# Earlier first logits and a new spread of gate steps and splits in the stick-breaking stage of a two-layer decoder trunk

## The chip, the cores and the metric

The kernel runs on one core of one Trainium2 chip. The metric is the device time of one execution in microseconds (us). Of each kernel one execution is also profiled; its trace has its own time and span, and all durations in this text come from such a trace.

The engines are TensorE (PE in the profile; its weight loads are PEld), VectorE (DVE), ScalarE (ACT), GpSimd (POOL) and SyncE (SP), which here only starts DMAs. PE writes to PSUM, eight banks of 128 x 512 floats; ACT and DVE read from there.

## The reference

Two layers over 512 tokens of width 2048, all in float32, batch 1. Layer 0 is a sparse attention chosen by an indexer; layer 1 is a stick-breaking attention with 16 query heads and 4 shared key/value heads of width 128. Each layer adds its mixer to the scaled stream, normalises it and adds a gated embedding. The change touches layer 1's mixer only:

```python
def mixer_b(x, w_in, w_o, k, v):
    q, gate = jnp.split(x @ w_in, [WIDTH_B], axis=-1)
    ...
        z = jnp.einsum('bqngd,bsnd->bngqs', qg, k).astype(jnp.float32) * (HEAD_DIM ** -0.5)
        strict = key_pos[None, :] < t[:, None]
        log_om = jnp.where(strict, -jax.nn.softplus(z), 0.0)
        suffix = lax.cumsum(log_om, axis=log_om.ndim - 1, reverse=True) - log_om
        a = jnp.where(strict, jnp.exp(jax.nn.log_sigmoid(z) + suffix), 0.0)
        o = jnp.einsum('bngqs,bsnd->bqngd', a.astype(v.dtype), v)
    ...
    return (o * jax.nn.silu(gate)) @ w_o
```

So the stage needs q and gate (two products of 2048 by 2048 weights), then for each of 4 key heads, with 4 query heads each, logits, a softplus, a running sum over the keys from the right, an exponential, and the product with the values.

## The kernel before

**Numbers.** Every float32 operand of PE is split into a high part (a rounded copy, made by ACT) and a low part (the rest, made by DVE: `split`, L140). A product is three matmuls, high x high, high x low and low x high (`mm3`, L145 to L147). So each new operand costs one ACT and one DVE instruction before PE can use it. Weights come from DRAM in pairs of 128 x 512 blocks into three buffers `raw`, in the order of the list `units`, by loads on SP's queue; each load waits until its buffer has been read. Their parts `wh` and `wl` have three buffers each, so a weight can be split at most three ahead of the one that PE uses.

**The stages around the change.** The queries (`F[0]` to `F[3]`, one per group of four heads) are made by a Strassen product in five chunks (`gemm_s`; the first chunk makes the values). A chunk has 112 steps of three matmuls of 128 x 256. Strassen overwrites half of the columns of eight blocks of the stream (`XH`, `XL`) by sums; these halves are read back from DRAM (`x2`) and split again (`restore`) in the next stage. During a chunk, small pieces of work wait in the list `bg`, and `pumped_at` takes one from it at the listed steps: the adds that end the chunk before, and in the last chunk the splits of the values (`split_values`) and of the first group's keys (`split_keys`). The last chunk ends with `combine_last`: one copy on ACT, seven adds on DVE.

**The stick-breaking stage** has four groups. In each, PE makes the gate of the group (`gemm_w` or `gate_first`: 16 weights, four steps each, 64 gate steps of three matmuls) and in between the attention of that group's four heads in ten units (`Sticks.units`), a unit being one block of 128 queries against one block of 128 keys. What a unit needs is spread over turns (`Sticks.turn`, L1369):

- `logits`: three matmuls into a PSUM bank (two banks alternate; unit 0 of a group has a third); in diagonal units a mask is added by DVE,
- `soft`: three instructions on ACT (absolute value, exponential, logarithm), `plus`: one on DVE; together the softplus,
- `high`, `low`: its two parts on DVE, with the running total of the block row put in; ACT copies a row `t` of the logits,
- `weights`: two matmuls add the running sum onto the logits; ACT takes the exponential, DVE updates the total; only then is the bank free for the logits two units on,
- `halves`: the two parts of the exponential (ACT, DVE), `values`: three matmuls with the values, `leave`: a copy of the output to `F` by ACT.

Turn s issues the logits and softplus of unit s, the values of unit s-2 and the weights of unit s-1, with `gate(n)` putting n gate steps in between (three numbers for each turn in `TURNS`). `feed()` splits gate weights ahead (up to ten gate steps beyond the current one unless told otherwise), `others(n)` takes n pieces from `bg`.

**What sets the order.** PE's order is the order of the code. On ACT and DVE a scheduler orders what is free to move; `paced` keeps pieces in program order, and `strictly` puts each instruction behind the last strict one of its engine. All of the stick-breaking stage is strict, so one late instruction on ACT or DVE holds all behind it. Instructions of ACT and DVE are all issued in a helper and carry its lines in the profile: L116 if strict, L118 if not; they are told apart by their tiles.

Group 0 starts like this (L1427 on): the query splits 3 and 1 are held back behind the combining adds, nine gate steps run, then come the logits of units 0 and 1 with one gate step between them.

```python
    bg.extend(lambda i=i: after_combining(split_scaled, 0, i) for i in (3, 1))
    ...
    for n in range(9):
        gate(1)
        if bg:
            one()
        feed()
    strictly(sticks.logits, 0)
    gate(1)
    strictly(sticks.logits, 1)
```

At the boundary of two groups, PE goes on with the logits of units 0 and 1 of the next group and ten gate steps, while ACT and DVE close the old group (`close`: SiLU and product), change the activation table, and start the new softplus chains.

Of the kernel before, what the change touches and what calls it, by code (L numbers as in the profile page):

```python
# [10 lines left out]
F32 = mybir.dt.float32  # L11
F32R = mybir.dt.float32r
I32 = mybir.dt.int32
AF = mybir.ActivationFunctionType
ALU = mybir.AluOpType
# [62 lines left out]
def trunk_kernel(  # L78
# [61 lines left out]
    def split(hi, lo, src, eng=dve):  # L140
        act.activation(hi, src, AF.Copy)
        eng.tensor_tensor(lo, src, hi.bitcast(F32), ALU.subtract)
# [217 lines left out]
    def one():  # L360
        paced(bg.popleft())

    def pumped_at(gen, when):
        for i, _ in enumerate(gen):
            if bg and i in when:
                one()
            yield
# [203 lines left out]
    for g in range(4):  # L571
        add_job(w_in_b, g * 512, strassen=True)
    x2 = dram.tile([D, T], F32, name="x2")
    for k in (4, 5, 6, 7, None, 0, None, 1, 2, 3):
        if k is None:
            first = 4 * (units[-1][1] == 0)
            units.append((x2.rearrange("(k p) t -> p k t", p=128)[:, first : first + 4, H:T],))
        else:
            units.append((w_in_b, 2 * k, 2 * k + 1, D, 512))
# [599 lines left out]
        split(XH[k][:, H:T], XL[k][:, H:T], raw[:, k % 4])  # L1179

    def gate_items():
        for k, n in ((0, 8), (4, 2)):
            yield from plain_items([(512, n)])
            raw = next_raw()
            bg.extend(lambda raw=raw, k=k: restore(raw, k) for k in range(k, k + 4))
            if k:
                bg.append(lambda: split_keys(1))
        yield from plain_items([(512, 6), *[(512, NK)] * 3])

    C3.extend(c3_tiles(pc_.enter_context(tc.tile_pool(name="pc1", bufs=1))))  # L1190
    V, K = ([tuple(spots[n : n + 2]) for n in where] for where in ((0, 2, 4, 6), (8, 14) * 2))
    Q, A = ([tuple(spots[n : n + 2]) for n in where] for where in ((10, 12, 16, 18), (20, 22)))

    def split_keys(g):
        split(*K[g], Kf[:, g])

    def split_values(t):
        split(*(v.rearrange("p (g d) -> p g d", g=4) for v in V[t]), Vf[:, :, t * 128 : (t + 1) * 128])

    with tc.tile_pool(name="sp", bufs=1) as sp:  # L1200
        Kf, Vf = shared
        banks = [bank(b, "k") for b in range(4)]
        gemm = gemm_w(kitems, plain, banks, order=PAIRS)
        items = first_chunk(gemm, TF, T1, C3, lambda: strassen_stream([512] * 5, sp))
        for g in range(4):
            act.activation(Kf[:, g], banks[g], AF.Copy)

        def turn_values(t):
            s = slice(t * 128, (t + 1) * 128)
            ps = bank(2, "vt")  # L1210
            for g in range(4):
                pe.transpose(ps[:, g * 128 : (g + 1) * 128], Vf[:, g, s], ident)
            act.activation(Vf[:, :, s], ps.rearrange("p (g d) -> p g d", g=4), AF.Copy)

        for n, dst in enumerate((Vf, *F)):
            M = product_banks(4 - n)
            gemm = pumped_at(gemm_s(items, C3, M), (13, 20, 27, 34, 41, 53, 65, 77, 89, 101))
            if n == 1:
                steps(gemm, 40)
                for t in range(4):  # L1220
                    steps(gemm, 16)
                    turn_values(t)
            run(gemm)
            drain()
            if n == 4:
                items = Ahead(gate_items(), 2).prime()
                combined = combine_last(sp, M, lambda i: quarter(dst, i))
            else:
                bg.extend(combine(sp, M, lambda i: quarter(dst, i)))
            if n == 3:  # L1230

                bg.extend(lambda t=t: split_values(t) for t in range(4))
                bg.append(lambda: split_keys(0))

    pv_.close()
    px = pc_.enter_context(ss(name="px", bufs=1))

    def split_scaled(g, i):
        qh, ql = (q.rearrange("p (h q) -> p h q", h=4) for q in Q[i])
        src = F[g][:, :, i * 128 : (i + 1) * 128]  # L1240
        act.activation(qh, src, AF.Copy, scale=HSCALE)
        dve.scalar_tensor_tensor(ql, src, HSCALE, qh.bitcast(F32), ALU.mult, ALU.subtract)

    def gate_first(banks):

# [21 lines left out]
    class Sticks:  # L1267
# [101 lines left out]
        def turn(self, s, gaps):  # L1369

            late = self.diagonal(s)
            new = 1 < s < 10
            if new:
                strictly(self.logits, s)
                if late:
                    strictly(self.low, s - 1)
                strictly(self.soft, s)
                if not late:
                    strictly(self.plus, s)
                    feed(1)  # L1380
            gate(gaps[0])
            if s > 1:
                strictly(self.values, s - 2)
            gate(gaps[1])
            if s < 11:
                strictly(self.weights, s - 1)
                if new and late:
                    strictly(self.plus, s)
                strictly(self.halves, s - 1)
                if new:  # L1390
                    strictly(self.high, s)
                    if not self.diagonal(s + 1):
                        strictly(self.low, s)
            else:
                strictly(act.preload_act_table_set, "silu_and_others")
            if s > 1:
                strictly(self.leave, s - 2)

            if self.g < 3:
                bg.extend(lambda i=i: split_scaled(self.g + 1, i) for i in {8 if self.g == 0 else 6: (1,), 9: (3,), 10: (0,)}.get(s, ()))  # L1400
            feed()
            others(1 if self.g else 2)
            gate(gaps[2])

    def after_combining(fn, *args):
        with tc.issue_after(combined):
            fn(*args)

    gated = [0]

    def gate(n):
        steps(gemm, n)
        gated[0] += n

    def feed(most=9, ahead=10):

        while most and items.count < min(64, -(-(gated[0] + ahead) // 4)):
            strictly(items.push)
            most -= 1

    def others(n):
        for _ in range(min(n, len(bg))):
            strictly(bg.popleft())

    LOG_EXP = "natural_log_exp_and_others"
    tc.keep_in_program_order(act.preload_act_table_set(LOG_EXP))
    bg.extend(lambda i=i: after_combining(split_scaled, 0, i) for i in (3, 1))  # L1427
    banks = mm_banks("g")
    items = Fed(items)
    gemm = gate_first(banks)  # L1430
    sticks = Sticks(0)
    for n in range(9):
        gate(1)
        if bg:
            one()
        feed()
    strictly(sticks.logits, 0)
    gate(1)
    strictly(sticks.logits, 1)
    for u in range(2):  # L1440
        for fn in (sticks.soft, sticks.plus, sticks.high, sticks.low):
            strictly(fn, u)
        feed(1)
    bg.extend(lambda i=i: split_scaled(0, i) for i in (2, 0))
    for n in (3, 2, 2):
        gate(n)
        feed()
        others(1)

    TURNS = (  # L1450
        ((0, 0, 2), (1, 1, 3), (1, 1, 2), (1, 1, 2), (2, 1, 2), (1, 1, 2), (1, 1, 3), (2, 1, 2), (1, 1, 2), (1, 1, 2), (1, 1, 3)),
        ((0, 0, 3), *[(1, 1, 3)] * 3, (2, 1, 3), *[(1, 1, 3)] * 2, (2, 1, 3), (1, 1, 3), (1, 1, 2), (1, 1, 4)),
    )
    for g in range(4):
        for s in range(1, 12):
            if g and s == 2:
                bg.append(lambda g=g: split_scaled(g, 2))
            if 0 < g < 3 and s == 3:
                bg.append(lambda g=g: split_keys(g + 1))
            sticks.turn(s, TURNS[g > 0][s - 1])  # L1460
        gate(64 * (g + 1) - gated[0])
        others(len(bg))
        if g < 3:
            then = Sticks(g + 1)
            for u in range(2):
                strictly(then.logits, u)

        def close(h):
            sg = work()
            act.activation(sg, banks[h], AF.Silu)  # L1470
            dve.tensor_tensor(F[g][:, h], F[g][:, h], sg, ALU.mult)

        for h in range(4):
            strictly(close, h)
        if g < 3:
            sticks = then
            feed(1)
            strictly(act.preload_act_table_set, LOG_EXP)
            for u in range(2):
                for fn in (sticks.soft, sticks.plus, sticks.high, sticks.low):  # L1480
                    strictly(fn, u)
                feed(1)
            banks = mm_banks("g")
            gemm = gemm_w(items, plain, banks)
            for _ in range(5):
                gate(2)
                feed()
    pk_.close()
    pc_.close()

# [55 lines left out]
```

## Time and profile before

| what | us |
|---|---|
| median of 3 runs | 1875.55 (1875.39 to 1876.4) |
| profiled execution | 1875.82 |
| its span, first to last instruction | 1874.1 |
| PE busy | 1857.8 (99% of the span) |
| DVE busy | 1232.3 (66%) |
| ACT busy | 939.8 (50%) |

The mean granted clock of PE was 0.998. In the timeline of this trace the last Strassen matmul starts just before 1233.88, the first logits of group 0 at 1240.03, those of groups 1 to 3 at 1305.66, 1369.28 and 1432.88, and the output projection at 1497.78.

A row of the timeline gives start, duration, engine, line, operation, what is written and read, the shape, and in brackets how long the engine sat idle before it and which instruction ended that. `c` stands for all tiles cut from one big buffer: keys, values, queries and the halves of the exponential. `z` are logits, `wk` work tiles, `sh` and `sl` the parts of the softplus, `g` the gate's banks, `o` the output's. A row of the table of stretches gives the stretch, its length, the busy time of PE, PEld, DVE, ACT and POOL with the number of instructions, the granted clock, the busy share of the DMA engines, and GB/s. The table of waits gives total, times and longest. Matmuls overlap: one is shown with about 0.39 us while the next starts 0.23 after it.

### The profile page before, as it was taken

To read this page: it belongs to the slowest core of one execution; us is meant where nothing else is said; L and a number is where in the kernel's file an instruction comes from. 1 tells how busy PE (TensorE), PEld (TensorE's weight loads), DVE (VectorE), ACT (ScalarE), POOL (GpSimd) and SP (SyncE) were. 2 spreads that over 40 slices of the span, in tenths; PEclk is the share of its full clock that TensorE was granted. 3 is DMA by queue.
4 is the path that set the end of the run, shared out by engine and by line. 5 is a ranking of instruction groups with operands and counts; after the bars stand their busy time and mean duration, and the time that the engine had idled before them with its cause. 6 is when DMAs were issued, how large, how long until landed. Compare 5 with 4: busy or idle time off the path is not lost.

```text
span 1874.1 us, 24812 instructions
## 1 busy us (share of the span) xinstructions
PE 1857.8 (99%) x9181; PEld 1576.2 (84%) x9181; DVE 1232.3 (66%) x2395; ACT 939.8 (50%) x1696; POOL 4.7 (0%) x20
## 2 busy tenths in 40 slices
PE   9999999999999999999999999999999999999998
PEld 8898888888888888888888999987777888888887
DVE  5668678566556454675367788877877745567534
ACT  3546333355554432474245444468888743347422
POOL 0000000000000000000000000000000000000000
PEclk9999999999999999999999999999999999999999
DMA  6441333322222532333343333322122253243333
GB/s 197 127 121 60 102 91 101 92 66 68 68 68 66 162 110 79 124 102 108 117 133 116 104 100 111 103 79 79 56 68 71 71 185 101 73 129 94 120 101 113
DMA packets 111178, 189.21 MB, mean 101 GB/s; under 512 B 8528, under 2 KB 29008, under 8 KB 111056
## 3 DMA queue, kind: packets, MB, share of 16 engines
q1 hardware_dynamic: 111056, 187.62, 32.9%
q8 instruction: 72, 1.18, 0.3%
q14 instruction: 50, 0.41, 0.1%
HBM read 179.21 MB, written 8.39 MB: 100 GB/s over the span
## 4 chain that ended last, share of the span: by engine, by line
PE 93%; ACT 3%; DVE 2%; issue 1%; DMA 0%; SPq 0%; DVEq 0%; ACTq 0%
PE g L145 11%; PE g L147 11%; PE g L146 11%; PE o L145 7%; PE o L147 7%; PE o L146 7%; PE m L145 4%; PE m L147 4%; PE m L146 4%; PE q L145 3%; PE q L147 3%; PE q L146 3%; ACT wk L116 2%; PE k L147 2%; PE k L146 2%; PE k L145 2%
## 5 line engine op out<-in xcount | busy, mean ns | idle before, releaser
L118 ACT ACTIVATE wh<-raw 128x512 fp32r<-128x512 f32 (+2 forms) x624 | 359.5, 577 | 688.4 <-PE g L146 220.4
L118 DVE TENSOR_TENSOR wl<-raw,wh 128x512 fp32r<-128x512 f32 (+2 forms) x624 | 388.2, 623 | 439.6 <-ACT wh L118 424.9
L145 PE MATMUL g<-xh,wh 128*128 128x512 f32 x1024 | 404.3, 395 | 3.6 <-ACT wh L116 3.6
L147 PE MATMUL g<-xh,wl 128*128 128x512 f32 x1024 | 400.3, 391 | 0.0
L146 PE MATMUL g<-xl,wh 128*128 128x512 f32 x1024 | 399.9, 390 | 0.0
L147 PEld LDWEIGHTS g<-xh,wl 128*128 128x128 f32 x1024 | 192.5, 188 | 42.4 <-DVE wl L116 1.3
L145 PEld LDWEIGHTS g<-xh,wh 128*128 128x128 f32 x1024 | 192.8, 188 | 41.7 <-ACT wh L116 4.8
L146 PEld LDWEIGHTS g<-xl,wh 128*128 128x128 f32 x1024 | 192.8, 188 | 37.0
L146 PE MATMUL o<-xl,wh 128*128 128x512 f32 x512 | 199.2, 389 | 0.0
L145 PE MATMUL o<-xh,wh 128*128 128x512 f32 x512 | 199.2, 389 | 0.0
L147 PE MATMUL o<-xh,wl 128*128 128x512 f32 x512 | 199.2, 389 | 0.0
L147 PEld LDWEIGHTS o<-xh,wl 128*128 128x128 f32 x512 | 96.1, 188 | 20.1
L146 PEld LDWEIGHTS o<-xl,wh 128*128 128x128 f32 x512 | 96.1, 188 | 20.0
L145 PEld LDWEIGHTS o<-xh,wh 128*128 128x128 f32 x512 | 96.1, 188 | 19.9
L145 PE MATMUL q<-xh,wh 128*128 128x512 f32 x256 | 99.6, 389 | 0.0
L146 PE MATMUL q<-xl,wh 128*128 128x512 f32 x256 | 99.6, 389 | 0.0
L147 PE MATMUL q<-xh,wl 128*128 128x512 f32 x256 | 99.6, 389 | 0.0
L118 ACT ACTIVATE sh<-st 128x512 fp32r<-128x512 f32 x80 | 49.7, 624 | 44.2 <-DVE st L118 44.1
L116 ACT ACTIVATE wk<-z 128x512 f32<-128x512 f32 x80 | 47.6, 595 | 38.6 <-DVE z L116 16.2
L118 DVE TENSOR_TENSOR sl<-st,sh 128x512 fp32r<-128x512 f32 x80 | 55.1, 690 | 13.9 <-ACT sh L118 13.9
L118 DVE TENSOR_TENSOR xl<-f,xh 128x512 fp32r<-128x512 f32 x80 | 54.3, 685 | 12.6 <-ACT f L118 12.3
L147 PEld LDWEIGHTS q<-xh,wl 128*128 128x128 f32 x256 | 48.1, 188 | 10.0
(297 smaller groups left out, 3394.2 us busy)
## 6 DMA issues: line engine op xcount, KB each, us to landing
raw<-w_in_a SPq DMA_DIRECT2D x95, 512.0 KB, 3.7
raw<-w_in_b SPq DMA_DIRECT2D x64, 512.0 KB, 3.8
raw<-w_ple_gate SPq DMA_DIRECT2D x52, 512.0 KB, 3.7
raw<-w_o_a SPq DMA_DIRECT2D x24, 512.0 KB, 3.7
raw<-w_o_b SPq DMA_DIRECT2D x24, 512.0 KB, 3.7
raw<-w_kv_b SPq DMA_DIRECT2D x16, 512.0 KB, 3.8
raw<-w_ple_gate SPq DMA_DIRECT2D x24, 256.0 KB, 2.9
f<-xT SPq DMA_DIRECT2D x4, 1024.0 KB, 6.4
```

What stands on the lines that cost most here:

```text
L116: ins = method(*args, **kw)
L118: ins = method(*args, **kw)
L145: pe.matmul(out, a[0], b[0], start=start, stop=False)
L146: pe.matmul(out, a[0], b[1], start=False, stop=False)
L147: pe.matmul(out, a[1], b[0], start=False, stop=stop)
```

## The change

Seven edits, all around the stick-breaking stage.

1. The logits of unit 0 stand first in group 0, before any gate step; then come six gate steps, the logits of unit 1, five gate steps, and the turns.
2. The query splits 3, 1 and 2 of group 0 become pieces of the last Strassen chunk, pumped at steps 104, 107 and 110, behind the values and keys. Query part 3 moves to buffers that the chunk reads last in its fourth of eight rounds; part 0 takes the old buffers of part 3 and is split in turn 1.
3. All groups use one list `TURNS` of mostly five gate steps a turn. Group 0 had its own of mostly four.
4. `first_soft` puts a weight split (`feed(1, ahead)`) between the softplus of units 0 and 1 and their high and low parts, in all groups. At the boundaries the ten gate steps follow without feeds of their own.
5. In turns of diagonal units (5 and 8) only one weight is fed, and nothing is taken from `bg`.
6. The read-back of the first four half blocks from `x2` comes after three pairs of gate weights instead of four, the second after two more pairs instead of one.
7. `after_combining` goes.

```diff
-    for k in (4, 5, 6, 7, None, 0, None, 1, 2, 3):
+    for k in (4, 5, 6, None, 7, 0, None, 1, 2, 3):
...
-        for k, n in ((0, 8), (4, 2)):
+        for k, n in ((0, 6), (4, 4)):
...
-    Q, A = ([tuple(spots[n : n + 2]) for n in where] for where in ((10, 12, 16, 18), (20, 22)))
+    Q, A = ([tuple(spots[n : n + 2]) for n in where] for where in ((18, 12, 16, 10), (20, 22)))
...
-            gemm = pumped_at(gemm_s(items, C3, M), (13, 20, 27, 34, 41, 53, 65, 77, 89, 101))
+            gemm = pumped_at(gemm_s(items, C3, M), (13, 20, 27, 34, 41, 53, 65, 77, 89, 101, 104, 107, 110))
...
                 bg.append(lambda: split_keys(0))
+                bg.extend(lambda i=i: split_scaled(0, i) for i in (3, 1, 2))
...
-            feed()
-            others(1 if self.g else 2)
+            if new and late:
+                feed(1)
+            else:
+                feed()
+                others(1 if self.g else 2)
             gate(gaps[2])
...
+    def first_soft(u, ahead=18):
+        strictly(sticks.soft, u)
+        strictly(sticks.plus, u)
+        feed(1, ahead)
+        strictly(sticks.high, u)
+        strictly(sticks.low, u)
+
...
-    bg.extend(lambda i=i: after_combining(split_scaled, 0, i) for i in (3, 1))
...
-    for n in range(9):
-        gate(1)
-        if bg:
-            one()
-        feed()
     strictly(sticks.logits, 0)
-    gate(1)
-    strictly(sticks.logits, 1)
-    for u in range(2):
-        for fn in (sticks.soft, sticks.plus, sticks.high, sticks.low):
-            strictly(fn, u)
-        feed(1)
-    bg.extend(lambda i=i: split_scaled(0, i) for i in (2, 0))
-    for n in (3, 2, 2):
-        gate(n)
-        feed()
-        others(1)
-
-    TURNS = (
-        ((0, 0, 2), (1, 1, 3), (1, 1, 2), (1, 1, 2), (2, 1, 2), (1, 1, 2), (1, 1, 3), (2, 1, 2), (1, 1, 2), (1, 1, 2), (1, 1, 3)),
-        ((0, 0, 3), *[(1, 1, 3)] * 3, (2, 1, 3), *[(1, 1, 3)] * 2, (2, 1, 3), (1, 1, 3), (1, 1, 2), (1, 1, 4)),
-    )
+    for u, n in enumerate((6, 5)):
+        for _ in range(n):
+            gate(1)
+            if not u:
+                feed()
+        if not u:
+            strictly(sticks.logits, 1)
+            first_soft(0)
+            first_soft(1, 14)
+    bg.append(lambda: split_scaled(0, 0))
+
+    TURNS = ((0, 0, 3), *[(1, 1, 3)] * 3, (2, 1, 3), *[(1, 1, 3)] * 2, (2, 1, 3), (1, 1, 3), (1, 1, 2), (1, 1, 3))
...
             for u in range(2):
-                for fn in (sticks.soft, sticks.plus, sticks.high, sticks.low):
-                    strictly(fn, u)
-                feed(1)
+                first_soft(u)
             banks = mm_banks("g")
             gemm = gemm_w(items, plain, banks)
-            for _ in range(5):
-                gate(2)
-                feed()
+            gate(10)
```

More of the change, by code (lines that the diff above doesn't have):

```diff
@@ L1198, in split_values, with split_scaled @@
         split(*(v.rearrange("p (g d) -> p g d", g=4) for v in V[t]), Vf[:, :, t * 128 : (t + 1) * 128])
+    def split_scaled(g, i):
+        qh, ql = (q.rearrange("p (h q) -> p h q", h=4) for q in Q[i])
+        src = F[g][:, :, i * 128 : (i + 1) * 128]
+        act.activation(qh, src, AF.Copy, scale=HSCALE)
+        dve.scalar_tensor_tensor(ql, src, HSCALE, qh.bitcast(F32), ALU.mult, ALU.subtract)
     with tc.tile_pool(name="sp", bufs=1) as sp:
@@ L1233, in trunk_kernel @@
                 bg.append(lambda: split_keys(0))
+                bg.extend(lambda i=i: split_scaled(0, i) for i in (3, 1, 2))
     pv_.close()
     px = pc_.enter_context(ss(name="px", bufs=1))
[L1238 to L1242, printed above, removed]
     def gate_first(banks):
@@ L1400, in turn @@
                 bg.extend(lambda i=i: split_scaled(self.g + 1, i) for i in {8 if self.g == 0 else 6: (1,), 9: (3,), 10: (0,)}.get(s, ()))
-            feed()
-            others(1 if self.g else 2)
+            if new and late:
[3 more added lines that the diff above has]
+                others(1 if self.g else 2)
             gate(gaps[2])
-    def after_combining(fn, *args):
-        with tc.issue_after(combined):
-            fn(*args)
     gated = [0]
@@ L1459, in trunk_kernel @@
                 bg.append(lambda g=g: split_keys(g + 1))
-            sticks.turn(s, TURNS[g > 0][s - 1])
+            sticks.turn(s, TURNS[s - 1])
         gate(64 * (g + 1) - gated[0])
```

## The prediction

> **What bounds the kernel now.** I read the page's head first, then a table of stretches over the stick-breaking stage, then the list of waits of PE, and last the timelines of PE, DVE and ACT around the places that these named.
>
> ```profile
> span 1874.1 us, 24812 instructions
> ...
> PE 1857.8 (99%) x9181; PEld 1576.2 (84%) x9181; DVE 1232.3 (66%) x2395; ACT 939.8 (50%) x1696; POOL 4.7 (0%) x20
> ```
>
> TensorE is the bound: a change that leaves the matmuls as they are can only win what PE loses between them. A busy matmul hides part of that, so I count starts. These two rows stand 23 matmuls apart (one turn of five gate steps: 15 gate, 3 logits, 2 weights, 3 values), in a turn without a wait:
>
> ```profile
> 1323.01 0.39 PE L145 MATMUL z<-c 128*128 128x512 f32 x1
> ...
> 1328.22 0.39 PE L145 MATMUL z<-c 128*128 128x512 f32 x1
> ```
>
> 5.21 / 23 = 0.2265 us for each. A group of four heads has 64 x 3 gate matmuls and 10 x 8 of the sticks, 272, so it needs at least 61.7. The four groups, from the last Strassen matmul to the first matmul of the output projection:
>
> ```profile
> core 0: us, PE busy (x) PEld busy (x) DVE busy (x) ACT busy (x) POOL busy (x), PEclk, DMA share, GB/s
> 1233.88:1305.66 71.78, 66.16 (x275) 51.48 (x273) 55.32 (x95) 52.57 (x94) 1.23 (x6) 0.98 0.25 74
> 1305.66:1369.28 63.62, 62.61 (x274) 50.69 (x272) 50.00 (x82) 51.62 (x88) 0.00 (x0) 1.00 0.22 67
> 1369.28:1432.88 63.60, 62.59 (x274) 50.70 (x272) 50.01 (x82) 51.63 (x88) 0.00 (x0) 1.00 0.22 67
> 1432.88:1497.78 64.90, 62.93 (x274) 50.65 (x272) 50.14 (x81) 51.81 (x88) 0.00 (x0) 1.00 0.21 65
> ```
>
> Less 61.7 each, they lose 10.1, 1.9, 1.9 and 3.2: **17.1 us in all**, the most that this change can win here. The reader sees also that ACT and DVE need 50 to 55 us a group, not much less than PE, so their order decides. The waits behind the loss:
>
> ```profile
> PE g L145 <- ACT wh L116: 3.6, 3, 1.8
> PE z L145 <- DVE t L116: 3.2, 3, 1.8
> PE o L1359 <- ACT c L116: 1.7, 1, 1.7
> ```
>
> The first row is three group boundaries, the other two are group 0. The third has a sequel, a stretch at a lower granted clock:
>
> ```profile
> 1249.78:1257.50 7.72, 5.57 (x16) 3.79 (x15) 5.95 (x10) 6.00 (x11) 0.00 (x0) 0.78 0.41 116
> ```
>
> 15 matmuls start in it, 3.4 us at full pace, so 4.3 are lost at one place; 0.22 x 7.72 = 1.7 of them by the clock.
>
> **Part 1, the first chain of group 0.** Before, PE does nine gate steps, the logits of unit 0, one more step, and the logits of unit 1.
>
> ```profile
> 1237.10 0.68 DVE L118 TENSOR_TENSOR f<-f,m 128x512 f32<-128x512 f32 x1
> 1237.69 0.22 DVE L118 CAST down<-wk 128x128 fp32r<-128x128 f32 x1
> ...
> 1240.98 0.70 DVE L116 TENSOR_TENSOR z<-z,gone 128x512 f32<-128x512 f32 x1
> ...
> 1243.74 0.69 DVE L116 SCALAR_TENSOR_TENSOR wk<-z,wk 128x512 f32<-128x512 f32 x1 [0.76 <-ACT wk L116]
> 1244.46 0.43 DVE L116 CAST sh<-wk 128x512 fp32r<-128x512 f32 x1
> 1244.92 0.69 DVE L116 TENSOR_TENSOR sl<-wk,sh 128x512 fp32r<-128x512 f32 x1
> ```
>
> The last combining add starts at 1237.10 and the next DVE instruction 0.59 later. With the logits ahead of the gates (0.68 on PE, from 1233.88) the mask waits only for the combining: it starts at 1237.84 behind the cast, 3.1 earlier than now. From mask to softplus is 2.76 (1240.98 to 1243.74): plus at 1240.60. The change now puts a weight split between plus and high part. Its ACT half waits for the second weight to be used up (about 1240.65) and takes 0.63, its DVE half then takes a slot of 0.6 from 1241.34: high part 1241.94, low part 1242.40 to 1243.09. PE comes to the weights of unit 0 after two logits and 11 gates, 2 x 0.68 + 11 x 0.68 = 8.84, at 1242.72; its second matmul is due at 1242.95 and waits to about 1243.15: 0.3 with the restart. Then the old big wait:
>
> ```profile
> 1241.78 0.60 ACT L116 ACTIVATE wk<-z 128x512 f32<-128x512 f32 x1 [1.82 <-DVE z L116]
> ...
> 1248.39 0.63 ACT L116 ACTIVATE wh<-raw 128x512 fp32r<-128x512 f32 x1
> ...
> 1250.61 0.60 ACT L116 ACTIVATE wk<-z 128x512 f32<-128x512 f32 x1
> 1251.23 0.63 ACT L116 ACTIVATE c<-wk 128x512 fp32r<-128x512 f32 x1
> ```
>
> From 1248.39 to 1250.61 ACT splits two weights and two queries ahead of the exponential of unit 0. In the new order only the rest of unit 1's chain stands there (its softplus ends at 1243.9, its total row at 1245.2): exponential 1245.2, high half 1245.87 to 1246.50, low half on DVE to 1247.3. Its values are due on PE at 1246.85, the matmul that needs the low half at 1247.30: no wait. So the 4.3 go, 0.3 comes.
>
> **Part 2, five gate steps a unit.** The ten turns of group 0 have 47 gate steps, now 54; 11 stand before them instead of 17.
>
> ```profile
> 1280.61 0.50 PE L145 MATMUL z<-c,c 128*128 128x512 f32 x1 [1.75 <-DVE t L116]
> ```
>
> Logits s wait until the bank of unit s-2 has been read by ACT's exponential and DVE's total; between that unit's weights and these logits stand two gates now, three after the change (0.68 more). Groups 1 and 2 run with three already and lose 0.3 and a restart at one such place:
>
> ```profile
> 1344.32 0.39 PE L147 MATMUL g<-xh,wl 128*128 128x512 f32 x1
> 1344.85 0.50 PE L145 MATMUL z<-c 128*128 128x512 f32 x1
> ```
>
> Group 0 has eight half-width restores more than they have. Walking its turns with the slots above, the restores (0.35 a slot on ACT and DVE, two a turn) and the weight behind plus cost 0.1 at logits 3, 0.6 at logits 4 and 0.7 at logits 7; with the 0.3 of part 1 and 0.3 for small ones **group 0 keeps 2.0 of 10.1**. Bounds: 0, or 6.0 if all its logits waits stay (10.1 less the 4.1 of part 1).
>
> **Part 3, weights at the boundaries.** Of 1.9 in groups 1 and 2, the most is one wait for the fourth weight of a group:
>
> ```profile
> 1316.66 0.50 PE L145 MATMUL g<-xh,wh 128*128 128x512 f32 x1 [0.87 <-ACT wh L116]
> ```
>
> ```profile
> 1312.06 0.59 ACT L116 ACTIVATE t<-z 32x512 f32<-32x512 f32 x1 [0.76 <-DVE wk L116]
> ...
> 1315.98 1.15 ACT L116 ACTIVATE wh<-raw 128x512 fp32r<-128x512 f32 x2
> 1317.15 0.60 ACT L116 ACTIVATE wk<-z 128x512 f32<-128x512 f32 x1
> ```
>
> ACT idles 0.76 ahead of each total row because DVE's plus has to go first; the new order puts a weight into each of these two holes, instead of both at 1315.98. On ACT that is free and the exponential comes 1.15 earlier; on DVE it puts 0.6 ahead of the high part (low part ready 1313.85, due on PE about 1314.05: free), and in unit 1 ahead of the first low half (ready 1318.35 against 1318.1 due). With restarts the boundary loses 0.35 for 1.4: **0.85 left of 1.9**. In diagonal turns one of two weights moves behind the next softplus; both still stand ahead of the exponential that releases the bank, so the 0.4 above stays. In group 3 a hoisted split waits for PE:
>
> ```profile
> 1439.88 0.63 ACT L118 ACTIVATE xh<-f 128x512 fp32r<-128x512 f32 x1 [0.90 <-PE g L147]
> ```
>
> It still stands in ACT's order, so I take only 0.9 there: **2.3 left of 3.2** (bounds 0.85 and 3.2).
>
> **Parts at nothing.** Three query splits move into Strassen's last chunk, behind its last weights and keys: three ACT slots of 0.52, three DVE slots of 0.6.
>
> ```profile
> 1228.00:1233.88 5.88, 5.88 (x51) 5.88 (x50) 3.35 (x6) 3.07 (x6) 0.00 (x0) 1.00 0.31 90
> ```
>
> DVE is free for 2.5 there, ACT for 2.8; the need is 1.8 and 1.6, and the tiles they overwrite were last read in chunk steps 55 to 83 of 112. Without that cover they cost up to 2.0 (3 x 0.68). The fourth query split goes into turn 1, where nothing waits. The load of x2 and of one pair of weights change places on SP's queue: the pair starts when the fourth weight is split (about 1239.7),
>
> ```profile
> raw<-w_in_b SPq DMA_DIRECT2D x64, 512.0 KB, 3.8
> ```
>
> lands 3.8 later and is first wanted in turn 2, near 1251; on SP only the next load stands behind it, which needs a later slot. If that failed the price would be 3.8.
>
> **The sum.** Left: 2.0 + 0.85 + 0.85 + 2.3 = 6.0; won 17.1 - 6.0 = 11.1. The profiled execution took 1875.82 (its span and 1.7 around it), 0.27 over the median of the runs. 1875.82 - 11.1 = **1864.7**.
>
> [...] The 0.78 row puts the slow clock behind 1.75 us of idle PE. [...]
>
> **The rivals.** (a) Group 0 stays bound by DVE and ACT: 55.3 and 52.6 us of work must fit into 63.7, and the logits waits stay (6.0 left, not 2.0): 1868.7. For it: DVE's load, 5 over groups 1 and 2. Against: those run 5-gate turns with one small wait. (b) All waits go: 1875.82 - 17.1 = 1858.7. [...] (d) The change doesn't do what it says: the third query split is placed behind the combining as now, and the logits at PE's head wait from 1233.88 to 1238.5, 4.6, with a slow clock of 1.7: 1871.0. Against: the free 2.5 above. (e) Slower: weights behind plus hold up the release of every bank by one DVE slot, 0.6 in each of 40 turns, 24.0, with 2.7 at starts and boundaries 26.7 lost for 17.1: 1885.4. It decides from (17.1 + 3.75 - 2.7) / 40 = 0.45 a turn. Against: groups 1 and 2 split as many weights a turn and lose 0.4 in ten.
>
> **How the numbers follow.** Mine 0.55 (1861.5 to 1868), a 0.15, b 0.05, c 0.07, d 0.08, e 0.10. This kernel's measurement tells 0.2%, 3.75 us, from no change: faster means under 1871.8. Faster: mine, a, b, c and half of d, 0.86, taken as 0.85; same 0.05; slower 0.10. The range 1860.5 to 1872 leaves out e and most of b.
>
> **What would show it.** The first z matmul directly behind the last Strassen one without a gap; its mask near 1237.8; no wait of o on ACT and a clock of 1.00 throughout; groups of about 63.7, 62.5, 62.5 and 64.0. A wait of z on DVE in every turn, a gap at the head, or idle over 0.3 in Strassen's last chunk would make it wrong.

## The result and the profile after

The changed kernel takes **1867.0 us** (median, 1866.57 to 1867.76), the kernel before, measured beside it, 1875.49 (1874.28 to 1876.4): a ratio of 0.9955, with a 95% interval of 0.9941 to 0.997. The forecast was 1864.7, in a range of 1860.5 to 1872: the right direction, 8.5 us won where 10.8 were forecast against the median.

Head of the profiled execution, 1867.0 us long, then the table of stretches over the four groups, with the columns explained above:

```profile
span 1865.3 us, 24806 instructions
...
PE 1855.9 (99%) x9181; PEld 1575.5 (84%) x9181; DVE 1231.2 (66%) x2395; ACT 939.0 (50%) x1696; POOL 4.7 (0%) x20
```

```profile
1234.03:1299.02 64.99, 63.91 (x275) 50.15 (x273) 53.14 (x91) 50.30 (x90) 1.24 (x6) 1.00 0.28 81
1299.02:1362.26 63.24, 62.65 (x272) 50.85 (x273) 49.73 (x82) 51.98 (x89) 0.00 (x0) 1.00 0.23 67
1362.26:1424.99 62.73, 62.27 (x273) 50.82 (x272) 49.89 (x82) 51.50 (x88) 0.00 (x0) 1.00 0.23 68
1424.99:1488.99 64.00, 63.11 (x274) 50.69 (x273) 49.95 (x81) 51.67 (x88) 0.00 (x0) 1.00 0.21 66
```

The last row ends 0.03 behind the first matmul of the output projection (1488.96). The span fell by 8.8. The four groups together take 254.93 where they took 263.90, so the stick-breaking stage gives all of it: 6.8 in group 0, 0.4, 0.9 and 0.9 in the others. PE is busy 1.9 us less with the same matmuls; the rest of the gain is idle time that went. Over the floor of 61.7 a group, 3.3, 1.5, 1.0 and 2.3 are left, 8.1 together, where 6.0 were forecast. The waits of PE in this stage (total, times, longest):

```profile
PE o L1362 <- DVE c L116: 1.1, 3, 0.5
PE z L145 <- DVE t L116: 1.0, 4, 0.4
PE z L145 <- ACT f L116: 0.5, 1, 0.5
PE z L1338 <- DVE sl L116: 0.2, 1, 0.2
PE g L147 <- DVE wl L116: 0.2, 1, 0.2
```

The three rows shown of before are gone or small: no `g` waits on ACT, `z` on DVE has 1.0 instead of 3.2, and `o` no longer waits on ACT. New is the first row, the low half of the first exponential, late by 0.2 to 0.5 us at each boundary. The first chain in the timeline of DVE:

```profile
1237.84 0.22 DVE L118 CAST down<-wk 128x128 fp32r<-128x128 f32 x1
1237.98 0.69 DVE L118 TENSOR_TENSOR z<-z,gone 128x512 f32<-128x512 f32 x1
...
1240.72 0.69 DVE L116 SCALAR_TENSOR_TENSOR wk<-z,wk 128x512 f32<-128x512 f32 x1 [0.25 <-ACT wk L116]
1241.50 0.69 DVE L116 TENSOR_TENSOR wl<-raw,wh 128x512 fp32r<-128x512 f32 x1
1242.11 0.42 DVE L116 CAST sh<-wk 128x512 fp32r<-128x512 f32 x1
1242.56 0.69 DVE L116 TENSOR_TENSOR sl<-wk,sh 128x512 fp32r<-128x512 f32 x1
```

The whole stage begins 0.15 later than in the trace before (1234.03 against 1233.88). With that taken off, mask, `plus`, high and low part start within 0.03 us of the times that the prediction wrote down.

### The profile page after: what moved, and what is told of

Same layout as the page of the kernel before. It is cut to its first block, busy times and chain, and to the rows that moved or that the text cites. A ratio compares the mean times of both kernels' runs of the same rounds, so it can differ in the third digit from the quotient of the medians.

```text
span 1865.3 us, 24806 instructions
## 1 busy us (share of the span) xinstructions
PE 1855.9 (99%) x9181; PEld 1575.5 (84%) x9181; DVE 1231.2 (66%) x2395; ACT 939.0 (50%) x1696; POOL 4.7 (0%) x20
## 4 chain that ended last, share of the span: by engine, by line
PE 93%; ACT 3%; DVE 2%; issue 1%; DMA 0%; SPq 0%; DVEq 0%; ACTq 0%
PE g L145 11%; PE g L147 11%; PE g L146 11%; PE o L147 7%; PE o L146 7%; PE o L145 7%; PE m L145 4%; PE m L147 4%; PE m L146 4%; PE q L145 3%; PE q L147 3%; PE q L146 3%; ACT wk L116 2%; PE k L146 2%; PE k L147 2%; PE k L145 2%
```

## The experiments

| kernel | group 0 | group 1 | group 2 | group 3 | median, us |
|---|---|---|---|---|---|
| before, trace shown | 71.78 | 63.62 | 63.60 | 64.90 | 1875.49 |
| before, a second trace | 70.14 | 63.62 | 63.64 | 64.80 | 1873.87, one execution |
| changed | 64.99 | 63.24 | 62.73 | 63.97 | 1867.00 |
| early first logits alone | 67.56 | 63.62 | 63.56 | 66.48 | 1872.74 |
| five-gate turns alone | 76.94 | 64.18 | 63.63 | 66.44 | 1882.71 |
| five-gate turns, new loads | 69.92 | 64.13 | 63.63 | 64.82 | 1875.16 |
| new loads alone | 71.50 | 63.59 | 63.59 | 64.86 | 1875.11 |
| changed, old loads | 77.41 | 63.31 | 62.74 | 64.00 | 1879.19 |
| changed, old boundary | 64.94 | 64.26 | 63.67 | 64.95 | 1870.33 |
| changed, old diagonal turns | 65.28 | 63.15 | 62.70 | 63.91 | 1866.74 |
| changed, second split later | 64.98 | 63.10 | 62.57 | 63.77 | 1866.16 |
| both of the last two | 65.28 | 63.00 | 62.42 | 63.71 | 1866.43 |

The groups are read from one trace each, from first logits to first logits (group 0 from its first matmul, group 3 to the first matmul of the output projection). Six of them hold stretches at a low granted clock, each worth 1.6 to 2.3 us: group 0 of the first row, of the turns alone, of the new loads alone and (two) of the changed kernel with old loads, and group 3 of the early logits alone and of the turns alone. A restart is what PE loses besides the idle time of a wait: the next matmul starts some 0.34 after the late one instead of 0.23.

**1. The early first logits alone** (edits 1, 2 and 7 on the kernel before; its turns, boundaries and loads stay).

```diff
+    strictly(sticks.logits, 0)
-    for n in range(9):
+    for n in range(6):
...
-    strictly(sticks.logits, 0)
-    gate(1)
...
-    bg.extend(lambda i=i: split_scaled(0, i) for i in (2, 0))
-    for n in (3, 2, 2):
+    bg.append(lambda: split_scaled(0, 0))
+    for n in (5, 3, 3):
```

> The kernel before with only its head changed: first logits ahead of the gate steps, query splits 3, 1 and 2 in the last Strassen chunk, then 6 gate steps, the logits of unit 1, and 11 gate steps; its own four-gate turns, boundaries and load order stay. Measured by the length of group 0, from the last Strassen matmul to the first logits of group 1: 71.8 before, 65.0 after, floor 61.7. My theory (the first chain's wait and the four-gate turns are two separate losses): the 4.3 at the first values go, the logits waits of the later turns stay, group 0 takes 67 to 68 and the kernel 1871 to 1872. Rival 1 (the late first chain is the whole cause): about 65, and 1869. Rival 2 (the turns are the whole cause): 71.8, no change. Groups 1 to 3 stay at 63.6, 63.6 and 64.9 under all.

Measured: 1872.74 (1871.32 to 1873.0), 0.9987 of before (0.9978 to 0.9997). Group 0 is 4.2 shorter than in the trace shown of before, the forecast's 4.1 of part 1, and 2.6 shorter than in a trace of before without a slow stretch (number 4). Group 0 lies where this run's forecast had it; the kernel is 0.7 over the forecast, and the profiled execution has a slow stretch in group 3, worth 1.6. The waits of PE say what goes and what stays: no `o` on ACT, and the other two rows as before.

```profile
PE g L145 <- ACT wh L116: 3.6, 3, 1.8
PE z L145 <- DVE t L116: 3.1, 3, 1.7
PE z L1338 <- DVE sl L116: 0.2, 1, 0.2
```

**2. The five-gate turns alone** (the start keeps its nine gates, then one gate instead of seven before the turns).

```diff
-    for n in (3, 2, 2):
+    for n in (1,):
...
-        others(1)
+        others(2)
...
-        ((0, 0, 2), (1, 1, 3), (1, 1, 2), ...
+        ((0, 0, 3), *[(1, 1, 3)] * 3, (2, 1, 3), ...
```

> The kernel before with only group 0's gate steps moved: 11 before the turns instead of 17, and the five-gate turns; the first logits stay behind nine gate steps. My theory: PE comes to the first weights near 1242.7 while the parts of the softplus are ready near 1245.6, so about 3 are lost there, and more at the first values; the later turns lose 1 to 2; group 0 takes 69 to 71 of 71.8 before, the kernel 1873 to 1875. Rival 1 (the late first chain is the whole cause, turns do not matter): 72 to 74. Rival 2 (the turns are the whole cause): about 66, the kernel 1870.

Measured: 1882.71 (1882.32 to 1883.12), 1.004 of before (1.0025 to 1.0055), 8 us over the median of before beside it (1874.67). Group 0 was forecast at 69 to 71 and takes 76.94. One wait of PE is longer than any of before's, and ACT's timeline says what it waits for, a weight still on its way from DRAM:

```profile
PE z L145 <- DVE t L116: 5.6, 1, 5.6
```

```profile
1278.27 0.63 ACT L116 ACTIVATE wh<-raw 128x512 fp32r<-128x512 f32 x1 [4.35 <-DMA raw<-w_in_b]
```

No row of before has a DMA as releaser here. That pointed to the edit that the prediction had priced at nothing, the load order. Numbers 5 to 7 test it.

**3. The old boundary in the changed kernel** (edit 4 undone at the boundaries, kept in group 0).

```diff
-                first_soft(u)
+                for fn in (sticks.soft, sticks.plus, sticks.high, sticks.low):
+                    strictly(fn, u)
+                feed(1)
...
-            gate(10)
+            for _ in range(5):
+                gate(2)
+                feed()
```

> The changed kernel with the boundaries of groups as before: no weight between plus and high part of the first two units, feeds between the ten gate steps. My theory: the wait for the fourth weight of each group comes back; groups 1 to 3 go from 63.2, 62.7 and 64.0 back to about 63.6, 63.6 and 64.9, the kernel is 1.5 to 2.5 slower than the changed one (1868.5 to 1869.5). Rival (the boundary's price is set by the chain of the first units, not by the weight): within 0.5 of the changed kernel.

Measured: 1870.33 (1869.49 to 1871.47), 3.3 over the changed kernel; groups 1 to 3 are 1.02, 0.94 and 0.98 longer, and the old wait is back:

```profile
PE g L145 <- ACT wh L116: 3.9, 3, 1.8
```

So the boundary's share of the gain is 2.9 us by the traces, with 1.0 won at each of the three. The 3.3 of the medians, more than forecast, holds more: four of the eight executions lie at 1869.49 to 1869.83, the profiled one among them, and four at 1870.82 to 1871.47.

**4. The kernel before once more,** with no edit, for its clock.

> The kernel before, for another profile. My theory (the slow clock follows the wait at the first values): the stretch from the first values' wait shows a granted clock near 0.78 over 7.7 again and group 0 takes 71.8. [...]

Measured: 1873.87, with the granted clock at 1.00 throughout. Group 0 takes 70.14, and not the 71.8 of my theory. The wait that stood ahead of the slow stretch is there to a hundredth, the slow stretch is not. PE's timeline in the second trace, and then in the one of the prediction:

```profile
1251.58 0.50 PE L1359 MATMUL o<-c,c 128*128 128x512 f32 x1 [1.74 <-ACT c L116]
...
1255.09 0.39 PE L146 MATMUL g<-xl,wh 128*128 128x512 f32 x1
1255.32 0.39 PE L147 MATMUL g<-xh,wl 128*128 128x512 f32 x1
```

```profile
1251.92 0.50 PE L1359 MATMUL o<-c,c 128*128 128x512 f32 x1 [1.75 <-ACT c L116]
...
1255.07 0.63 PE L145 MATMUL g<-xh,wh 128*128 128x512 f32 x1
1255.49 0.63 PE L146 MATMUL g<-xl,wh 128*128 128x512 f32 x1
```

Matmuls start 0.23 apart in the first and 0.42 in the second. The group is 1.64 shorter without the stretch. Of 20 executions of the kernel before that were timed in one later series, nine lie from 1873.71 to 1874.57 and eleven from 1875.22 to 1875.96, none between; that the two traces stand for the two clusters fits their times, but was not read in each.

**5. The old load order in the changed kernel** (edit 6 undone).

```diff
-    for k in (4, 5, 6, None, 7, 0, None, 1, 2, 3):
+    for k in (4, 5, 6, 7, None, 0, None, 1, 2, 3):
...
-        for k, n in ((0, 6), (4, 4)):
+        for k, n in ((0, 8), (4, 2)):
```

> The changed kernel with the load order of before (the first read-back of x2 after four pairs of gate weights, the second one pair later). In the run with the moved turns alone, PE lost 5.7 at one place behind a weight whose load could start only when the weight before it was split. My theory: that order no longer fits five-gate turns; the eleventh weight (turn 6) stands on ACT ahead of unit 5's exponential and waits 1.5 to 3 for its load, logits 7 come late: group 0 takes 66.5 to 69 instead of 65.0 and the kernel 1868.5 to 1871. Rival (my prediction's price of nothing for the order): 65.0 within 0.3, and 1867.

Measured: 1879.19 (1877.9 to 1879.73), 1.0022 of before (1.0012 to 1.0031): this single edit turns the whole gain into a loss, 12.2 us. All of it is in group 0 (77.41 against 64.99). The forecast had the place, the eleventh weight and logits 7, but only 1.5 to 4 of the loss: it had neither the second late load nor the slow stretches. The waits of PE, and ACT's and SP's timelines:

```profile
PE g L146 <- DVE xl L116: 4.9, 2, 2.4
PE z L145 <- DVE t L116: 3.3, 4, 2.6
PE z L145 <- ACT c L116: 1.6, 1, 1.6
```

```profile
1268.88 0.61 ACT L116 ACTIVATE wh<-raw 128x512 fp32r<-128x512 f32 x1
...
1273.91 0.63 ACT L116 ACTIVATE wh<-raw 128x512 fp32r<-128x512 f32 x1 [2.61 <-DMA raw<-w_in_b]
...
1282.88 0.63 ACT L116 ACTIVATE wh<-raw 128x512 fp32r<-128x512 f32 x1 [4.05 <-DMA raw<-w_in_b]
```

```profile
1255.52 0.37 SPq L198 DMA_DIRECT2D raw<-x  x1
1270.25 24.84 SPq L212 DMA_DIRECT2D raw<-w_in_b  x4
```

The two read-backs hold two of the three buffers `raw`. The next pair of weights can then only go into the third, and its load starts at 1270.25, as soon as DVE has made the low part of the weight that lay there:

```profile
1269.53 0.69 DVE L116 TENSOR_TENSOR wl<-raw,wh 128x512 fp32r<-128x512 f32 x1
```

It lands 3.7 later, ACT stands for it, and everything strict behind it on ACT and DVE is late: the exponential that frees the bank for `z`, and the restored halves `xl`. In the changed kernel the read-back goes first, and the pair's load starts ten microseconds sooner, when a restore has emptied a buffer:

```profile
1239.89 8.57 SPq L212 DMA_DIRECT2D raw<-w_in_b  x2
1256.29 0.37 SPq L198 DMA_DIRECT2D raw<-x  x1
1260.12 34.03 SPq L212 DMA_DIRECT2D raw<-w_in_b  x6
```

Why the same order does no harm in the kernel before is seen in ACT's timeline of its trace, at the tenth, and then the eleventh and twelfth weight of group 0:

```profile
1265.81 0.62 ACT L116 ACTIVATE wh<-raw 128x512 fp32r<-128x512 f32 x1
...
1275.70 1.13 ACT L116 ACTIVATE wh<-raw 128x512 fp32r<-128x512 f32 x2
```

There too the pair's load starts as soon as the tenth weight is split (1267.44), but the eleventh is only taken 9.9 after the tenth, so the 3.7 of the load are covered. The early logits alone, with four-gate turns and this order, keep that distance (1261.45 and 1271.33) and have no such wait. With five-gate turns ACT is ready for the eleventh weight 2.4 after the tenth here (1268.88 and 1271.30) and 0.6 after it in number 2, and stands.

From the starts of the matmuls, the four largest waits (2.76, 2.62, 2.72 and 1.73, each from start to start less the usual 0.23) make 9.8, and two slow stretches behind them 3.9 more. One of the two, in the table of stretches:

```profile
1280.00:1284.00 4.00, 4.00 (x11) 3.03 (x11) 0.89 (x2) 0.63 (x1) 0.00 (x0) 0.50 0.78 261
```

**6. Five-gate turns with the new load order,** number 2 with edit 6 added.

> The kernel before with group 0's gate steps moved as in the run with the turns alone, and the new load order. My theory: the 5.7 at the load and the slow clock behind it go; what is left is the late first chain, 2.8 at the first weights and 2.6 at the first values, and about 1 in the turns; group 0 takes 68 to 70 (76.9 with the turns alone, 70.1 before without a slow stretch), the kernel 1872.5 to 1874.5. Rival (the wait was not the load's but the turns' own): group 0 stays over 75 and the kernel over 1880.

Measured: 1875.16 (1874.07 to 1876.44), 1.0001 of before (0.9991 to 1.001), 7.5 under number 2. Group 0 takes 69.92, as forecast, and only 0.2 less than in the second trace of before; the profiled execution took 1874.22. The longest wait of the later logits is down from 1.75 to 1.1, by the 0.68 of one gate step that part 2 of the prediction has, but the start costs more than it did, since only two gate steps stand between the logits of unit 0 and their weights (one on either side of the logits of unit 1; before there were eight):

```profile
PE z L1337 <- ACT t L116: 2.2, 1, 2.2
PE o L1359 <- ACT c L116: 1.8, 1, 1.8
PE z L145 <- DVE t L116: 1.1, 1, 1.1
```

So the six gates that the turns gain have to come from somewhere; taken from behind the first logits they open a hole there, and in the changed kernel the early logits close it.

**7. The new load order alone** in the kernel before.

> The kernel before with nothing changed but the order of the loads of x2 and of one pair of gate weights (edit 6). The trace of before has no idle time of ACT that ends with a DMA in group 0, so if the old order only fails once the waits ahead of it are gone, the new one wins nothing here: 1875 to 1876, group 0 within 0.3 us of 70.1 (or 71.8 with a slow stretch). If the loads cost something in the old kernel too, hidden in its waits of the logits, group 0 falls by 1 us or more and the time to 1874 or less.

Measured: 1875.11 (1873.42 to 1876.73), 1.0 of before (0.999 to 1.0009). Group 0 takes 71.50 in this trace, with a slow stretch. In the kernel before the order of the loads is worth nothing.

**8. The old diagonal turns** (edit 5 undone).

```diff
-            if new and late:
-                feed(1)
-            else:
-                feed()
-                others(1 if self.g else 2)
+            feed()
+            others(1 if self.g else 2)
```

> The changed kernel with the diagonal turns feeding weights and taking pieces as all other turns do. My theory (both weights stand ahead of the exponential that frees the bank, wherever the second goes): the groups stay at 65.0, 63.2, 62.7 and 64.0 within 0.3 each, the kernel at 1867 within 0.7. Rival (the second weight ahead of the softplus delays logits 7): 0.4 to 0.6 more in each group, the kernel 1869.

Measured: 1866.74 (1866.66 to 1866.88), 0.9956 of before (0.994 to 0.9972), as the changed kernel. One wait of 1.1 of `z` on `t` in group 0 takes the place of several small ones, and of the 0.5 on `f` at the end:

```profile
PE z L145 <- DVE t L116: 1.4, 2, 1.1
PE o L1362 <- DVE c L116: 1.0, 3, 0.5
```

**9. The split behind the second softplus held back at the boundaries,** to take away the new wait on the low half.

```diff
-                first_soft(u)
+                first_soft(u, 14 if u else 18)
```

> The changed kernel, at the boundaries without the second unit's weight between plus and high part; turn 1 feeds it instead. My theory: that weight's low part on DVE is what makes the low half of unit 0 late (the values of unit 0 wait 0.37, 0.23 and 0.47 with restarts); the waits go, the groups 1 to 3 take 62.6, 62.2 and 63.2 instead of 63.2, 62.7 and 64.0, the kernel 1865 to 1866. Rival 1 (another instruction makes the half late): no change. Rival 2 (the weight is then late at its own gate step): groups 1 to 3 longer by 0.5 or more.

Measured: 1866.16 (1866.05 to 1866.23), 0.9952 of before (0.9939 to 0.9965). The row of `o` on DVE is gone, but groups 1 to 3 win only 0.14, 0.16 and 0.20 each, where the waits with their restarts were 0.64, 0.50 and 0.74 and the forecast was 0.5 to 0.8. In group 1 the stretch from logits 2 to logits 3, with the wait in it, is 0.36 shorter (5.53 for 5.89), and the one behind it 0.18 longer (5.39 for 5.21), spread over short delays that no row of waits shows. It is the fastest kernel of the study.

**10. Numbers 8 and 9 together.**

> The changed kernel with the second unit's weight split of the boundary held back and the old feeding of the diagonal turns. If the two add up: 1866.16 - 0.26 = 1865.9. If the diagonal turns' difference is noise: 1866.2. If the weights come too late for the gates: a wait of a gate matmul on a weight, and more than 1866.7.

Measured: 1866.43 (1866.17 to 1866.61), 0.9956 of before (0.9941 to 0.9971): the difference of the diagonal turns doesn't add up, so it is none.

## Why the prediction was right, and where it was off

**What bounds the kernel: right.** The same matmuls run, and the gain is lost time of PE in this stage. The stage won 9.0, the span 8.8.

**Part 1: the mechanism right, a part of its gain not the change's.** The timeline has each step within 0.2 us, the values no longer wait for the exponential (ACT starts it at 1245.41, forecast 1245.2), and the new wait at the weights is 0.29, forecast 0.3. But 1.7 of the 4.3 was the slow stretch, and number 4 shows that it doesn't come each time that the wait does. Against a trace without it the chain is worth 2.6 (number 1). The forecast of 11.1 was taken from a trace that had the stretch; from the second trace it would have been 9.4, and the change won 6.9 against it (1873.87 to 1867.0). That the stretch comes at its hour whatever the waits isn't shown either: the four kernels whose waits are all under 1.2 (the changed one and numbers 8 to 10) have none in this stage, and their executions lie 0.2 to 1.2 apart, where those of the five kernels with a wait of 1.7 to 2.2 and none longer (before, numbers 1, 3, 6 and 7) lie 1.7 to 3.3 apart.

**Part 2: the term that was mis-sized.** Group 0 keeps 3.3, not 2.0. Logits 4 lose 0.65 (forecast 0.6), logits 7 only 0.25 (0.7), the others named 0.3 (0.4). Not foreseen was the end of the group: the first logits of group 1 wait for ACT's copy of the last output,

```profile
1298.14 0.39 PE L147 MATMUL g<-xh,wl 128*128 128x512 f32 x1
1299.02 0.50 PE L145 MATMUL z<-c,c 128*128 128x512 f32 x1 [0.49 <-ACT f L116]
```

0.75 with the restart. Eleven gates and the 54 of the turns are 65, one more than there are, so the last turn has two gates where its list says three; I counted 54 and didn't ask which is cut. That the missing gate, 0.68, would have covered the 0.49 is argued, not tried. ACT makes that copy behind two query splits and a table load of 1.28 us; in number 8 one of these splits stands elsewhere, the copy comes 0.53 sooner after the values (2.20 for 2.73), and the wait is gone. The rest are small waits and restarts, some 1.3, one of them on a weight's low part (0.46). The direction of rival (a), a group 0 still held by DVE and ACT, has a third of its price: 1.3 of the 4.0 that lie between 2.0 and 6.0.

**Part 3: the right place, a slot short.** The wait for the fourth weight is gone at all three boundaries. In its stead comes the one that the prediction sized at 0.35 a boundary (the low half behind the split in unit 1), with 0.64, 0.50 and 0.74; groups 1 and 2 keep 1.5 and 1.0, not 0.85. Group 3 keeps 2.3 as forecast, but that is luck: the prediction took 0.9 off the wait for the weight, which is gone whole, 2.4 with its restarts, and 1.5 came new at the first weights and values. Number 9 takes the wait on the low half away and wins only a quarter to a third of it. The diagonal turns change nothing, as said (numbers 8 and 10).

**Parts at nothing: right for this change, wrong in what they are.** The query splits ride in Strassen's last chunk, three on ACT and three on DVE, and the `z` matmul stands directly behind the last Strassen one; rival (d) is out:

```profile
1228.09 1.66 ACT L118 ACTIVATE c<-f 128x512 fp32r<-128x512 f32 x3
```

```profile
1233.91 0.28 PE L147 MATMUL m<-c,wl 128*128 128x256 f32 x1
1234.03 0.40 PE L145 MATMUL z<-c 128*128 128x512 f32 x1
```

The swap of the loads was priced at nothing, and at 3.8 if it failed. The load does start when said (1239.89, forecast 1239.7) and nobody waits. But the swap isn't a free choice: without it the changed kernel loses 12.2 us (number 5), and the kernel before nothing (number 7). I asked whether the new order hurts, and not whether the old one would still do with five-gate turns, which bring the eleventh weight close behind the tenth. The step that was missing is the walk of SP's queue over group 0 in the new timing, buffer by buffer.

**Rivals (b) and (e): out.** No kernel came near 1858.7. Rival (e) also miscounted: in the turns of six units (all but the first two and the diagonal ones) the kernel before already has its weight split behind `plus` (the `feed(1)` of `Sticks.turn`, the same in both kernels). The change adds one behind `plus` only at the first two units of a group, seven in the trace, and groups 1 and 2 went down.

**The sum.** 8.1 left for 6.0 makes 2.1 of the 2.3 between 1864.7 and 1867.0; 0.15 is the later start of the stage. The slow stretch that the trace of before happened to have swells the forecast gain, 11.1 for 9.4, and not the forecast time: from the second trace it would be 1873.87 - 9.4 = 1864.5.

**The edits are not additive.** The early logits alone win about 2 us, the turns alone lose 8 and with the new loads win nothing, the loads alone nothing; together, with the split behind `plus` in group 0, they win 4.3 (number 3, against 1874.67), and the boundary adds 3.3. Where the trace of group 0 has no slow stretch the same is seen: 70.14 before, 67.56 with the early logits, 69.92 with turns and loads, and 64.94 with all of them, 5.2 won where the parts make 2.8.

## What to carry to other kernels

When an edit moves work between turns, walk the queue of loads again in the new timing: a load that starts when a buffer comes free may have been covered by the old distance of two weights (here 9.9 us, then 2.4, for a load of 3.7), and an edit that looks like tidying can be what carries the gain. Edits that move the same few gate steps between places are costed together, since each alone may only move the hole. Before a loss behind a short wait is counted as the change's to win, take a second trace of the same kernel: here 1.64 us of a forecast of 11.1 came and went by itself.

## What the runs showed of the hardware

In the traces of this stage, 4 of the 18 waits of PE of 1.74 to 2.19 us were followed by a stretch at a granted clock of 0.50, with 0.42 between matmuls instead of 0.23, and 14 were not. The four are the 1.75 in the first trace of before (with 0.41 a little later), 1.8 in group 3 of numbers 1 and 2 (clock 0.96 over 1430 to 1470 in both), and 2.05 in number 7. In the first trace of before the clock is at 0.50 from 1253.9 to 1257.3, 3.4 us; in the second the wait at the same place, 1.74, has no such stretch behind it (number 4). In this stage all waits of 2.4 us and more were followed by one: 5.6 us in number 2 (clock 0.95 over 1240 to 1310), and in number 5 2.61 with 2.45 close behind, whose 0.50 row is shown there, and another of 2.45 (matmuls 0.42 to 0.43 apart from 1301.43 to 1304.42).
